# Reciprocal roots by GpSimd's power in a sparse attention, and a later spreading step in feed-forward norms, in a one-core decoder trunk

## Chip, cores and metric

One core of a Trainium2 chip runs the whole program in one launch. The metric is the device time of an execution in microseconds (us), as the median over runs. The engines are TensorE (PE; PEld is its weight load), VectorE (DVE), ScalarE (ACT), GpSimd (POOL) and SyncE (SP), which issues the loads.

## What is computed

A trunk of four layers over 256 tokens of 1024 features, in float32. Each layer is

```python
x = x + 0.5 * swiglu(rmsnorm(x, ffn1_norm[i]), ffn1_w_gu[i], ffn1_w_down[i])
h = rmsnorm(x, mix_norm[i])
x = x + mixer(h)        # 0 gated delta rule, 1 stick-breaking, 2 sparse attention, 0 again
x = x + 0.5 * swiglu(rmsnorm(x, ffn2_norm[i]), ffn2_w_gu[i], ffn2_w_down[i])
# rmsnorm(x, g) = x * rsqrt(mean(x*x) + 1e-6) * g
```

The sparse attention projects `h` to a query latent (384), a key latent (256), a rotary key (32) and an index key (64), and takes an rmsnorm of the query latent, the key latent and the index key. Index scores choose 64 keys of 256 for each query, and a softmax over those keys attends.

## The kernel before, in words

Everything lies transposed, features on the partitions and 256 tokens along the free axis. A float32 product is made of three passes on two-part operands (high part by a copy on ACT, `piece` L172, remainder by a subtraction on DVE, L173), so each 128x128 weight tile costs three matmuls of 256 columns. These are the "products" below. Weights come in chunks of 1 MB, each good for 48 products.

A norm's factor is not needed by the products: they run on `x` times the gain, and the factor of each token is multiplied in afterwards. `rstd` (L241) makes it in three steps: squares on ACT and three and a half additions on GpSimd; two small matmuls with a matrix of ones (the "sum", on PE) with the mean taken by DVE into `ms` (L256), and the reciprocal root `rsqrt` (L205) on DVE, one bit trick and three rounds of Newton's iteration, 10 instructions; then two transposes on PE that spread the two columns of the result over all partitions (`spread`, L234, recorded at `tr`, L56), and a copy of that by ACT to `rb` (L261). `rms_factor` (L749) and `rowbc` (L758) do the same for the three latents of the sparse attention, where one more copy on DVE (L756) puts the result into `fac`.

What is issued when is set by a planner written by hand. A side task (`rstd`, `factor`, `index_scores`, `attend` and so on) is a generator; what it yields is the time until its next step is due, in the planner's own count, which each matmul advances by its columns over 2400 (0.1067 for a product of 256 columns, L47). `pump` (L132) is called after each 6 products of a wide tile (0.64 in the count) and runs the steps that are due; `wait` (L147) runs steps, due or not, until a condition holds. So a yield of 4.6 puts 48 products between the sum and the spreading. Within that order a list scheduler still moves instructions that are not ready by its own estimate.

In a feed-forward stage (`ffn`, L313) 192 products of gate and up come before the first rows of the down projection. The task `rstd` is added at the start, so the sum stands after product 60; the factor is waited for after product 144 (L339). In the first feed-forward stage of all the task is added only after product 48.

In the sparse attention (`dsa`, L762) the norm's factor is waited for after 96 products (L972). Then come three factors: `fk` (index key; its spread row is needed by `index_keys`, L835, whose PE work is at L842), `fq` (query latent; not spread, it scales the index weights at L808) and `fkv` (key latent; its spread row is needed before the keys `K` of L1001). DVE then finds the 64 best keys (`select`, L886: eight rounds of a maximum search) and writes the mask `neg` (L903), for which `attend` (L921) waits.

Of the kernel before, what the change touches and what calls it, by code (L numbers as in the profile page):

```python
# [11 lines left out]
F32 = mybir.dt.float32  # L12
# [5 lines left out]
ALU = mybir.AluOpType  # L18
AX = mybir.AxisListType

P = 128
T = 256
# [13 lines left out]
class Bank:  # L36


    def __init__(self, k, t):
        self.k, self.nc, self.t, self.fresh = k, k.nc, t, True  # L40
# [25 lines left out]
class Trunk:  # L66

    def __init__(self, tc, ctx, a):
        self.tc, self.nc, self.a = tc, tc.nc, a
        nc = self.nc  # L70
        pool = lambda **k: ctx.enter_context(tc.tile_pool(**k))
        self.const = pool(name="const", bufs=1)
        self.raw = pool(name="raw", bufs=3)
        self.hip = pool(name="hi", bufs=10)
        self.lop = pool(name="lo", bufs=10)
        self.wk = pool(name="wk", bufs=2)

        pool(name="gap", bufs=1).tile([P, 8], F32, name="gap")
        self.big = pool(name="big", bufs=8)
        self.ps = pool(name="ps", bufs=4, space=bass.MemoryType.PSUM)  # L80
        self.side, self.now = [], 0.0
        self.act_set("silu_and_others")
        c = self.const
        self.x = c.tile([P, KT, T], F32, name="x")
        self.gains = c.tile([P, 13, KT], F32, name="gains")
        self.ones = c.tile([P, P], F32, name="ones")
        nc.gpsimd.memset(self.ones, 1.0)
        self.ident = c.tile([P, P], F32, name="ident")
        bf = c.tile([P, 2, P], BF16, name="bf")
        self.identb, self.scap = (bf[:, i] for i in range(2))  # L90
        hf = c.tile([P, 3, P], F16, name="hf")
        self.identh, self.identk, self.m1 = (hf[:, i] for i in range(3))
        self.consts = ((self.ident, a["ident"]), (bf, a["bf"]), (hf, a["hf"]))
        self.pad = c.tile([P, T], F32, name="pad")
        nc.gpsimd.memset(self.pad, 0.0)
        self.pcs = [c.tile([P, 2, 3 + T], F32, name="pc%d" % i) for i in range(2)]
        for pc in self.pcs:
            nc.gpsimd.memset(pc[:, :, :3], 0.0)

# [138 lines left out]
            b.tr(b.t[:, i * P:(i + 1) * P], c.to_broadcast([P, P]))  # L238
        return b

    def rstd(self, st):  # L241

        nc = self.nc
        sq = self.b8("sq")
        for j in range(4):
            nc.scalar.activation(sq[:, 2 * j:2 * j + 2], self.x[:, 2 * j:2 * j + 2], AF.Square)  # L246
        nc.gpsimd.tensor_add(sq[:, 0:2], sq[:, 0:2], sq[:, 2:4])  # L247
        nc.gpsimd.tensor_add(sq[:, 0:2], sq[:, 0:2], sq[:, 4:6])
        nc.gpsimd.tensor_add(sq[:, 0:2], sq[:, 0:2], sq[:, 6:8])
        nc.gpsimd.tensor_add(sq[:, 0], sq[:, 0], sq[:, 1])  # L250
        yield self.lat_sum
        b = self.bank()
        for t in range(2):
            b.mm(b.t[:, t * P:(t + 1) * P], sq[:, 0, t * P:(t + 1) * P], self.ones)
        a = self.small("ms", [P, 2])
        nc.vector.tensor_scalar(a, b.v4()[:, :2, 0], 1.0 / D, EPS, op0=ALU.mult, op1=ALU.add)  # L256
        y = self.rsqrt(a, 2)
        yield self.lat_newton
        s = self.spread([y[:, t:t + 1] for t in range(2)])
        rb = self.small("rb", [P, T])  # L260
        nc.scalar.activation(rb, s.t[:, :T], AF.Copy)  # L261
        st["rstd"], st["rb"] = y, rb
# [1 line left out]

    pool_lo = ()
    lag, width, burst = 1.0, 6, 5
    lat_sum, lat_newton = 5.2, 4.6
    dsa_width = 4
    g_key, g_val, g_qry, g_del, g_new, g_inv, g_out, g_mul = 9.0, 6.0, 6.0, 8.0, 2.8, 1.0, 7.5, 1.0
    s_qk, s_sp, s_att = 2.5, 5.5, 1.3  # L270
# [42 lines left out]
    def ffn(self, w, n, first=False, done=None):  # L313
        nc = self.nc
        if first:
            c0, xg = self.first_chunk(w[0, 0], n)
        else:
            c0, xg = None, self.norm_in(n)
        st = {}
        if not first:  # L320
            self.add(self.rstd(st))

        def gu(s):
            for f in range(2):
                order = range(KT) if first and s + f == 0 else None
                c = c0 if c0 and s + f == 0 else self.chunk(w[s, f], parts=4 if first and s == 0 else 1)
                if first and s == 0 and f:
                    for t, src in self.consts:
                        nc.sync.dma_start(t, src)
                e = self.w5("e")  # L330
                for m in range(2):
                    b = self.tile_wide(c, m, order=order)
                    nc.scalar.activation(e[:, m * T:(m + 1) * T], b.t[:, :T], AF.Copy)  # L333
                    nc.vector.tensor_add(e[:, m * T:(m + 1) * T], e[:, m * T:(m + 1) * T], b.t[:, T:])  # L334
                late.append(e)
                if first and s + f == 0:
                    self.add(self.rstd(st))
                if s > 0:
                    self.wait(lambda: "rb" in st)  # L339
                if "rb" in st:  # L340
                    while late:
                        acts.append(act(late.pop(0)))

        def act(e):
            e2 = e.rearrange("p (a b) -> p a b", b=T)
            nc.vector.tensor_mul(e2, e2, st["rb"][:, None, :].to_broadcast([P, 2, T]))  # L346
            nc.scalar.activation(e[:, :T], e[:, :T], AF.Silu)  # L347
            nc.vector.tensor_mul(e[:, T:], e[:, T:], e[:, :T])  # L348
            ah, al = self.w2("ah", F32R), self.w2("al", F32R, "wb")
            self.split(ah, al, e[:, T:])  # L350
            return ah, al

        late, acts = [], []
        self.scale = 0.5
        for s in range(NS):
            gu(s)
            if s == 1:
                acc = [self.bank() for _ in range(4)]
            if s > 0:
                self.rows(acc, self.chunk(w[s - 1, 2]), (acts.pop(0), acts.pop(0)), False)  # L360
        self.rows(acc, self.chunk(w[NS - 1, 2]), acts, True, done)
# [387 lines left out]
    def rms_factor(self, sq, n, ones, out):  # L749

        b = self.bank()
        for t in range(2):
            b.mm(b.t[:, t * P:(t + 1) * P], sq[:, t * P:(t + 1) * P], ones)
        m = self.small("ms", [P, 2])
        self.nc.vector.tensor_scalar(m, b.v4()[:, :2, 0], 1.0 / n, EPS, op0=ALU.mult, op1=ALU.add)
        self.nc.vector.tensor_copy(out, self.rsqrt(m, 2))  # L756

    def rowbc(self, y, r):  # L758
        s = self.spread([y[:, t:t + 1] for t in range(2)])
# [2 lines left out]
    def dsa(self, n):  # L762
        nc, a = self.nc, self.a
# [9 lines left out]
        self.act_set("natural_log_exp_and_others")  # L773
        self.split(wih, wil, wi)
        st, fl = {}, set()
        self.add(self.rstd(st))
        self.width = 12

        lat = self.b8("lat")
# [43 lines left out]
        def factor(name, i, srcs, n, ones, row):  # L823
            if len(srcs) > 1:
                nc.gpsimd.tensor_add(sq[:, srcs[0]], sq[:, srcs[0]], sq[:, srcs[1]])
            if len(srcs) > 2:
                nc.gpsimd.tensor_add(sq[:, srcs[0]], sq[:, srcs[0]], sq[:, srcs[2]])
            yield 1.0 + 0.8 * (len(srcs) - 1)
            self.rms_factor(sq[:, srcs[0]], n, ones, fac[:, i])
            yield self.lat_newton  # L830
            if row is not None:
                self.rowbc(fac[:, i], row)
            fl.add(name)
# [138 lines left out]
        self.wait(lambda: "rb" in st)  # L972
        latents(1, b1)
        self.add(factor("fk", 2, (3,), 64, ones64, fk), 1.5)
        self.add(index_keys())
        latents(0, b0)
        self.add(idx_weights())
        self.pump(1)
        self.add(factor("fq", 0, (0, 1, 2), 384, self.ones, None), 1.5)
        self.add(weights())  # L980
        pieces = self.chunk(a["dsa_qidx"], 1536, 384)
# [6 lines left out]
        self.add(select())  # L988
        latents(2, project(2))
        self.add(factor("fkv", 1, (4, 5), 256, self.ones, fkv), 1.5)  # L990
        project_q(0)
        pieces = self.chunk(a["dsa_uk"], 1536, 384)
# [218 lines left out]
```

## Time and profile before

| what | us |
|---|---|
| median of 3 runs | 2086.51 |
| lowest and highest run | 2069.57, 2087.42 |
| the profiled execution's own time | 2071.74 |
| span of that execution, first to last instruction | 2069.9 |

The profile is of one execution. A row of a timeline gives the start, the duration, engine, line, operation, what is written and read, and in brackets how long the engine had been idle before and what ended that. Equal neighbours are merged, with their count. Ends of matmuls are modelled: neighbouring products overlap in the record, and their spacing is read from their starts.

### The profile page before, as it was taken

To read this page: it belongs to the slowest core of one execution; us is meant where nothing else is said; L and a number is where in the kernel's file an instruction comes from. 1 tells how busy PE (TensorE), PEld (TensorE's weight loads), DVE (VectorE), ACT (ScalarE), POOL (GpSimd) and SP (SyncE) were. 2 spreads that over 40 slices of the span, in tenths; PEclk is the share of its full clock that TensorE was granted. 3 is DMA by queue.
4 is the path that set the end of the run, shared out by engine and by line. 5 is a ranking of instruction groups with operands and counts; after the bars stand their busy time and mean duration, and the time that the engine had idled before them with its cause. 6 is when DMAs were issued, how large, how long until landed. Compare 5 with 4: busy or idle time off the path is not lost.

```text
span 2069.9 us, 43693 instructions
## 1 busy us (share of the span) xinstructions
PE 2006.7 (97%) x17578; PEld 1975.3 (95%) x17578; DVE 1611.2 (78%) x3456; ACT 1306.9 (63%) x2804; POOL 160.6 (8%) x145
## 2 busy tenths in 40 slices
PE   8999899999999999999999998999999998999998
PEld 8999889999999989999999996999999998899998
DVE  7778898866787776877787788877787788988776
ACT  6666776655666666665666664766666667766664
POOL 1001311100000010100010013100010013111000
PEclk9999999999999999999999999999999999999999
DMA  7555223555455554555555542455555542235552
GB/s 260 200 189 182 103 104 127 176 190 185 164 204 197 190 183 146 178 198 196 191 183 201 187 153 79 150 198 201 186 185 202 186 181 105 101 123 181 186 200 86
DMA packets 52619, 353.93 MB, mean 171 GB/s; under 512 B 6976, under 2 KB 7872, under 8 KB 10688
## 3 DMA queue, kind: packets, MB, share of 16 engines
q1 hardware_dynamic: 52128, 350.49, 47.8%
q8 instruction: 137, 2.24, 0.4%
q10 hardware_dynamic: 288, 0.66, 0.1%
q14 instruction: 66, 0.54, 0.1%
HBM read 350.07 MB, written 1.05 MB: 170 GB/s over the span
## 4 chain that ended last, share of the span: by engine, by line
PE 79%; DVE 15%; ACT 4%; issue 2%; POOL 0%; DMA 0%; SPq 0%; ACTq 0%; DVEq 0%; POOLq 0%
PE bankG L43 52%; PE bankA L43 26%; DVE l L173 6%; ACT x L224 1%; PE bankA L56 1%; DVE kT L470 1%; ACT h L172 1%; DVE x L225 1%; DVE rs_t L213 1%; DVE rs_y L214 1%; DVE x L306 1%; DVE rs_t L212 1%; DVE qT L470 0%; DVE e L334 0%; DVE vT L470 0%
## 5 line engine op out<-in xcount | busy, mean ns | idle before, releaser
L43 PE MATMUL bankG<-x,h 128*128 128x256 f32 x7008 | 1256.5, 280 | 10.0 <-ACT x L224 6.8
L173 DVE TENSOR_TENSOR l<-r,h 128x512 fp32r<-128x512 f32 x1328 | 938.2, 713 | 396.7 <-ACT h L172 395.3
L172 ACT ACTIVATE h<-r 128x512 fp32r<-128x512 f32 x1328 | 821.9, 626 | 573.5 <-PE bankG L43 329.6
L43 PEld LDWEIGHTS bankG<-x,h 128*128 128x128 f32 x7008 | 1079.4, 189 | 12.4 <-ACT x L224 7.1
L43 PE MATMUL bankG<-x,l 128*128 128x256 f32 x3504 | 977.5, 279 | 0.0
L43 PEld LDWEIGHTS bankG<-x,l 128*128 128x128 f32 x3504 | 661.9, 189 | 0.2
L43 PE MATMUL bankA<-al,h 128*128 128x256 f32 x1408 | 389.6, 277 | 0.0
L43 PE MATMUL bankA<-ah,h 128*128 128x256 f32 x1408 | 389.6, 277 | 0.0
L43 PE MATMUL bankA<-ah,l 128*128 128x256 f32 x1408 | 389.5, 277 | 0.0
L43 PEld LDWEIGHTS bankA<-al,h 128*128 128x128 f32 x1408 | 265.1, 188 | 0.1
L43 PEld LDWEIGHTS bankA<-ah,h 128*128 128x128 f32 x1408 | 264.3, 188 | 0.1
L43 PEld LDWEIGHTS bankA<-ah,l 128*128 128x128 f32 x1408 | 264.3, 188 | 0.0
L334 DVE TENSOR_TENSOR e<-e,bankG 128x256 f32<-128x256 f32 x352 | 145.3, 413 | 1.8 <-ACT e L333 1.8
L333 ACT ACTIVATE e<-bankG 128x256 f32<-128x256 f32 x352 | 133.7, 380 | 9.1 <-PE bankG L43 8.5
L247 POOL TENSOR_TENSOR sq<-sq 128x512 f32<-128x512 f32 x12 | 15.7, 1304 | 1454.7 <-ACT sq L246 1454.7
L346 DVE TENSOR_TENSOR e<-e,rb 128x512 f32<-128x512 f32 x176 | 119.6, 684 | 0.0
L201 ACT ACTIVATE ah<-e 128x256 fp32r<-128x256 f32 x176 | 72.8, 418 | 23.0 <-DVE e L348 22.7
L347 ACT ACTIVATE e<-e 128x256 f32<-128x256 f32 x176 | 71.2, 405 | 5.8 <-DVE e L346 5.8
L43 PE MATMUL bankG<-oh,h 128*128 128x256 f32 x256 | 73.4, 287 | 0.1
L348 DVE TENSOR_TENSOR e<-e 128x256 f32<-128x256 f32 x176 | 72.8, 418 | 0.5 <-ACT e L347 0.5
L202 DVE TENSOR_TENSOR al<-e,ah 128x256 fp32r<-128x256 f32 x176 | 72.7, 417 | 0.5 <-ACT ah L201 0.5
L43 PE MATMUL bankG<-oh,l 128*128 128x256 f32 x256 | 71.2, 279 | 0.0
(290 smaller groups left out, 1683.7 us busy)
## 6 DMA issues: line engine op xcount, KB each, us to landing
r<-in_ffn SPq DMA_DIRECT2D x262, 1024.0 KB, 4.8
r<-in_gdn_in SPq DMA_DIRECT2D x32, 1024.0 KB, 4.8
r<-in_gdn_out SPq DMA_DIRECT2D x8, 1024.0 KB, 4.7
r<-in_sb_qk SPq DMA_DIRECT2D x8, 1024.0 KB, 4.9
r<-in_sb_v SPq DMA_DIRECT2D x4, 1024.0 KB, 4.8
r<-in_sb_out SPq DMA_DIRECT2D x4, 1024.0 KB, 4.8
r<-in_dsa_out SPq DMA_DIRECT2D x4, 1024.0 KB, 4.8
r<-in_dsa_in SPq DMA_DIRECT2D x3, 1024.0 KB, 4.8
```

The lines of the kernel that those rows point to most:

```text
L43: self.nc.tensor.matmul(out, lhsT, rhs, start=self.fresh, stop=stop, skip_group_check=True)
L56: self.nc.tensor.transpose(out, x, self.k.ident)
L172: self.nc.scalar.activation(h[:, :pw], src, AF.Copy)
L173: (self.nc.gpsimd if pool else self.nc.vector).tensor_sub(l[:, :pw], src, h[:, :pw].bitcast(F32))
L201: self.nc.scalar.activation(dh, src, AF.Copy)
L202: self.nc.vector.tensor_sub(dl, src, dh.bitcast(F32))
L212: nc.vector.tensor_mul(t, y, y)
L333: nc.scalar.activation(e[:, m * T:(m + 1) * T], b.t[:, :T], AF.Copy)
L334: nc.vector.tensor_add(e[:, m * T:(m + 1) * T], e[:, m * T:(m + 1) * T], b.t[:, T:])
L346: nc.vector.tensor_mul(e2, e2, st["rb"][:, None, :].to_broadcast([P, 2, T]))
L347: nc.scalar.activation(e[:, :T], e[:, :T], AF.Silu)
L348: nc.vector.tensor_mul(e[:, T:], e[:, T:], e[:, :T])
```

## The change

`rstd` gets two arguments, the planner's delay between sum and spreading, and whether the root is taken by one GpSimd instruction: `ms` to the power of -0.5, the exponent from two columns of a constant tile. The sparse attention's norm and its three factors use the power, with 2.4 as the delay. All other norms keep Newton's iteration; in the feed-forward stages the delay becomes 6.6 in place of 4.6, elsewhere it stays 4.6. The constant lies behind the data of one of the two convolution tiles, each of which grows by two columns.

```diff
-        self.pcs = [c.tile([P, 2, 3 + T], F32, name="pc%d" % i) for i in range(2)]
+        pcs = [c.tile([P, 2 * (4 + T)], F32, name="pc%d" % i) for i in range(2)]
+        self.pcs = [t[:, :2 * (3 + T)].rearrange("p (m t) -> p m t", m=2) for t in pcs]
+        self.half = pcs[1][:, 2 * (3 + T):]
+        nc.gpsimd.memset(self.half, -0.5)
...
-    def rstd(self, st):
+    def rstd(self, st, lat=4.6, power=False):
...
-        y = self.rsqrt(a, 2)
-        yield self.lat_newton
+        if power:
+            y = self.small("rs_y2", [P, 2])
+            nc.gpsimd.tensor_tensor(y, a, self.half, op=ALU.pow)
+        else:
+            y = self.rsqrt(a, 2)
+        yield lat
...
-    lat_sum, lat_newton = 5.2, 4.6
+    lat_sum, lat_power = 5.2, 2.4
...
-            self.add(self.rstd(st))                  # ffn, twice (L321, L337)
+            self.add(self.rstd(st, 6.6))
...
-        self.nc.vector.tensor_copy(out, self.rsqrt(m, 2))          # rms_factor
+        self.nc.gpsimd.tensor_tensor(out, m, self.half, op=ALU.pow)
...
-        self.add(self.rstd(st))                      # dsa
+        self.add(self.rstd(st, 2.4, True))
...
-            yield self.lat_newton                    # factor
+            yield self.lat_power
```

## Rows read from the trace of the kernel before

**Rows 1.** The page: the busy time of each engine with its share of the span and its instructions; then the busy time of each engine between 400 and 560 us, inside one feed-forward stage (engine, busy us, count; then TensorE's granted clock, the DMA share and GB/s).

```profile
PE 2006.7 (97%) x17578; PEld 1975.3 (95%) x17578; DVE 1611.2 (78%) x3456; ACT 1306.9 (63%) x2804; POOL 160.6 (8%) x145
...
400.00:560.00 160.00, 160.00 (x1360) 160.00 (x1360) 110.95 (x209) 93.78 (x189) 0.00 (x0) 1.00 0.53 186
```

**Rows 2.** The timeline of PE in feed-forward stages: in the second stage the sum, the last product ahead of the spreading and the spreading; then the spreading of the other six.

```profile
383.43 0.60 PE L43 MATMUL bankA<-ones,sq 128*128 128x128 f32 x4
...
389.21 0.28 PE L43 MATMUL bankG<-x,h 128*128 128x256 f32 x1
390.29 0.40 PE L56 MATMUL bankA<-ident,rs_y 128*128 128x128 f32 x2 [0.80 <-DVE rs_y L214]
...
578.53 0.43 PE L56 MATMUL bankA<-ident,rs_y 128*128 128x128 f32 x2 [0.72 <-DVE rs_y L214]
...
867.85 0.40 PE L56 MATMUL bankA<-ident,rs_y 128*128 128x128 f32 x2 [0.79 <-DVE rs_y L214]
...
1049.62 0.43 PE L56 MATMUL bankA<-ident,rs_y 128*128 128x128 f32 x2 [0.71 <-DVE rs_y L214]
...
1343.64 0.40 PE L56 MATMUL bankA<-ident,rs_y 128*128 128x128 f32 x2 [0.46 <-DVE rs_y L214]
...
1525.40 0.43 PE L56 MATMUL bankA<-ident,rs_y 128*128 128x128 f32 x2 [0.72 <-DVE rs_y L214]
...
1891.09 0.40 PE L56 MATMUL bankA<-ident,rs_y 128*128 128x128 f32 x2 [0.80 <-DVE rs_y L214]
```

**Rows 3.** The timeline of DVE in the second feed-forward stage: the mean, and the last of Newton's ten instructions.

```profile
386.88 0.15 DVE L256 TENSOR_SCALAR ms<-bankA 128x2 f32<-128x2 f32 x1
...
389.98 0.16 DVE L214 SCALAR_TENSOR_TENSOR rs_y<-rs_t,rs_y 128x2 f32<-128x2 f32 x1
```

**Rows 4.** What PE waited for in the sparse attention, 1228 to 1300 us, the seven longest: us in total, times, longest.

```profile
PE bankA L56 <- DVE fac L756: 3.3, 1, 3.3
PE bankA L43 <- DVE lat L839: 1.9, 1, 1.9
PE bankG L43 <- DVE l L173: 1.7, 1, 1.7
PE bankA L56 <- DVE p L940: 1.4, 3, 0.7
PE bankA L43 <- DVE qtmp L914: 0.9, 1, 0.9
PE bankG L43 <- DVE K L1001: 0.8, 1, 0.8
PE bankA L56 <- DVE rs_y L214: 0.6, 1, 0.6
```

**Rows 5.** The timeline of PE in the sparse attention: the norm's sum and spreading, `fk`'s sum, the first matmuls of `index_keys`, the sum and the spreading of `fkv`.

```profile
1225.16 0.71 PE L43 MATMUL bankA<-ones,sq 128*128 128x128 f32 x4 [0.22 <-POOL sq L250]
...
1230.71 0.43 PE L56 MATMUL bankA<-ident,rs_y 128*128 128x128 f32 x2 [0.60 <-DVE rs_y L214]
...
1233.73 0.60 PE L43 MATMUL bankA<-tab,sq 128*128 128x128 f32 x4
...
1247.49 1.52 PE L43 MATMUL bankA<-lat,tab 128*128 128x256 f32 x4 [1.86 <-DVE lat L839]
...
1259.34 0.60 PE L43 MATMUL bankA<-ones,sq 128*128 128x128 f32 x4
...
1269.99 0.40 PE L56 MATMUL bankA<-ident,fac 128*128 128x128 f32 x2 [3.27 <-DVE fac L756]
```

**Rows 6.** Three us behind the wait of 1.86 us, by the view of stretches (columns as in rows 1).

```profile
1248.00:1251.00 3.00, 3.00 (x14) 2.81 (x13) 1.71 (x5) 0.00 (x0) 2.34 (x3) 0.51 0.50 156
```

**Rows 7.** The three lines of Newton's iteration proper on DVE between 1227 and 1271 us, grouped by line: count, busy us, mean ns, idle before.

```profile
L213 DVE SCALAR_TENSOR_TENSOR rs_t<-rs_t,ms 128x2 f32<-128x2 f32 x12 | 4.0, 331 | 0.2
L214 DVE SCALAR_TENSOR_TENSOR rs_y<-rs_t,rs_y 128x2 f32<-128x2 f32 x12 | 3.5, 288 | 0.2
...
L212 DVE TENSOR_TENSOR rs_t<-rs_y 128x2 f32<-128x2 f32 x12 | 2.4, 202 | 0.3
```

**Rows 8.** The timeline of DVE in the sparse attention: the means of the norm, of `fk` and of `fkv`, one instruction of `fkv`'s Newton iteration, the start of `select` and its mask.

```profile
1227.59 0.15 DVE L256 TENSOR_SCALAR ms<-bankA 128x2 f32<-128x2 f32 x1
...
1234.37 0.16 DVE L755 TENSOR_SCALAR ms<-bankA 128x2 f32<-128x2 f32 x1
...
1261.17 0.15 DVE L755 TENSOR_SCALAR ms<-bankA 128x2 f32<-128x2 f32 x1
...
1264.31 1.24 DVE L213 SCALAR_TENSOR_TENSOR rs_t<-rs_t,ms 128x2 f32<-128x2 f32 x1
...
1269.76 0.48 DVE L891 TENSOR_TENSOR m<-m,tab 128x128 f32<-128x128 f32 x2
...
1286.59 0.48 DVE L903 SCALAR_TENSOR_TENSOR neg<-m,tab 128x128 bf16<-128x128 f32 x2
```

**Rows 9.** The timeline of POOL around `fkv`: the rotary parts of the queries.

```profile
1260.95 1.43 POOL L915 TENSOR_TENSOR Q<-Q,tab 32x512 f32<-32x512 f32 x1 [6.03 <-PE bankA L43]
1263.74 1.79 POOL L916 TENSOR_TENSOR Q<-Q,qtmp 32x512 f32<-32x512 f32 x1 [1.36 <-DVE qtmp L914]
```

**Rows 10.** POOL's instructions grouped by line: an addition of 256 columns, and the shortest instruction over 128 partitions in several columns.

```profile
L825 POOL TENSOR_TENSOR sq<-sq 128x256 f32<-128x256 f32 x2 | 1.5, 736 | 12.7 <-ACT sq L816 12.7
...
L98 POOL MEMSET pc<- 128x6 f32 x2 | 0.1, 105 | 0.0
```

More of the change, by code (lines that the diff above doesn't have):

```diff
@@ L336, in gu @@
                 if first and s + f == 0:
-                    self.add(self.rstd(st))
+                    self.add(self.rstd(st, 6.6))
                 if s > 0:
@@ L775, in dsa @@
         st, fl = {}, set()
-        self.add(self.rstd(st))
+        self.add(self.rstd(st, 2.4, True))
         self.width = 12
```

## The prediction

> **What bounds the kernel now.** I read the shares of the page first, then a stretch of a feed-forward stage, then what PE waited for, then timelines at each norm. PE is busy 97% of the span, and between 400 and 560 us it is busy for all 160.00 us at full granted clock, with DVE at 110.95 and ACT at 93.78 [rows 1]. So PE sets the pace there, and whatever keeps it idle for a moment is paid in full, unless a later wait is shortened by it. In seven feed-forward stages the one such moment is the norm's spreading: PE stands 0.80, 0.72, 0.79, 0.71, 0.46, 0.72 and 0.80 us for Newton's last instruction [rows 2]. That is 5.00 us. In the sparse attention PE is not fully busy. There a chain goes back and forth between PE, DVE and POOL, and the waits are larger: 3.3 us for `fkv`'s factor, 1.9 for the index key, 1.7 for a weight remainder, 1.4 for the softmax, 0.9 for a query's rotation, 0.8 for a key eviction, 0.6 for the norm [rows 4].
>
> **Feed-forward stages: the later spreading.** In the second stage the sum ends at 383.43 + 0.60 = 384.03, and the 48 products behind it end at 389.21 + 0.28 = 389.49, so one product takes 5.46 / 48 = 0.114 us [rows 2]. Newton's result is there at 389.98 + 0.16 = 390.14, or 6.11 us after the sum; 2.85 of them pass before DVE gets to the mean at 386.88 [rows 3], and the rest is its ten small instructions with the stream's own between them. With 66 products in front, the transposes come 66 x 0.114 = 7.52 us after the sum: 1.4 us later than the result, and the wait is gone. In the planner's count 6.6 / 0.64 gives 11 pumps, which is 66 products, where 4.6 / 0.64 gave 8. The sum stands after product 60, so the spreading comes after product 126, still ahead of the point at 144 where the factor is asked for; 18 products or 2.05 us remain for two transposes, 0.40 us in rows 2, and the copy to `rb`. The gate and up values are multiplied by `rb` only after 144, before and after. So nothing is late next. Nothing new is queued: the same transposes move past 18 products that don't need them, and no load moves.
>
> In the first stage of all, the sum comes after product 108 (48, one pump, then 5.2 / 0.64 or 9 pumps) and the wait at 144 forces the spreading before either delay has run out. I count no change there. Gain of this part: 5.0 us, bounded by 0 (if the scheduler put the transposes where they were) and 5.0.
>
> **The sparse attention: one instruction for eleven.** Removed are ten DVE instructions four times and three copies; the three lines of the iteration proper alone cost DVE 4.0 + 3.5 + 2.4 = 9.9 us [rows 7]. Added are four POOL instructions of two columns and one filling of two columns at the start, 0.105 us for six [rows 10] on an engine that is busy 8% of the span [rows 1]; two longer constant tiles cost nothing. The power itself is nowhere in this trace. From below, POOL's shortest instruction takes 0.105 us [rows 10]; from above, a two-input one of 512 columns took 1.79 [rows 9]; an ordinary one of 256 columns takes 0.74 [rows 10]. I take 0.4, nearer the small end, since there are two columns, and above it, since a power is more than an addition. Below nothing it can't be.
>
> Norm: the sum ends at 1225.87 [rows 5]; DVE, busy with remainders, gives the mean at 1227.74 [rows 8]; 2.4 / 0.64 gives 4 pumps, 24 products, so the transposes come 2.74 us after the sum, at 1228.6. The power has 0.86 us and nothing in front of it on POOL. The wait of 0.60 [rows 5] goes.
>
> `fk`: the sum ends at 1234.33 [rows 5], the mean is there at 1234.53 [rows 8], so 2.5 us are left for the power and the wait for it is nil. The spread key comes some 20 products earlier in the planner's order, and DVE, free of `fq`'s Newton, makes the index key at once. So PE's 1.86 us [rows 5] go. What followed that wait goes too: the granted clock was 0.51 from 1248 to 1251, the 1.2 GHz level, after PE had idled until 1247.49 [rows 5, 6]. 14 products started in those 3 us [rows 6], where 3 / 0.114 = 26 do at full clock: (26 - 14) x 0.114 = 1.4 us lost. Behind the waiting power on POOL stand `fq`'s two additions, some 0.5 us later; `fq`'s sum is not asked for until some 20 products on.
>
> `fkv`: the sum ends at 1259.94 [rows 5], the mean at 1261.32 [rows 8]. POOL is in L915 until 1262.38 [rows 9], so the power ends at 1262.8, against transposes at 1259.94 + 2.74 = 1262.68: the wait of 3.27 us [rows 5] nearly vanishes. But POOL works in order. If the power is placed behind L916, which itself waits for DVE and ends at 1265.53 [rows 9], PE waits about 3.2 us again. No row shows which, so I take 2.0 us of the 3.27. Whatever stands behind the power on POOL (the queries' rotations) waits for the mean as well; `attend` needs them, 20 us later.
>
> Will the end of the stage follow? `neg` is written at 1286.59 + 0.48, at the end of a DVE chain that starts at 1269.76 [rows 8], 17 us of almost gapless DVE work. It starts earlier by what DVE saves in front of it and by the earlier index key, about the same 6 us as PE. So I move the rest along: neither the 1.7 nor the 1.4 of rows 4 goes or grows.
>
> Sum: 0.60 + 1.86 + 1.4 + 2.0 = 5.9 in the sparse attention and 5.0 in the feed-forward stages, 10.9 us. Against the profiled execution's own 2071.74 (1.84 outside its span of 2069.9) that is 2060.8. The median of the runs shown is 2086.51, 14.8 above that execution and 17 above the lowest run. I carry the saving over: 2086.5 - 10.9 = **2075.6 us**.
>
> *A rule against it.* DVE's instruction at 1264.31 took 1.24 us where its like takes 0.16 [rows 3], and it ended with POOL's L916, at 1265.5 [rows 8, 9]. The Trainium skill, "SBUF — State Buffer", section "Who interferes with whom", says that a DVE instruction with two SBUF inputs and a GpSimd instruction that reads SBUF exclude each other, the later one waiting in full. The trace agrees in this row. By the rule each power can be held up by DVE, and hold DVE up in turn; with the 1.08 us of this row at `fkv`, the one place without room, the sum would be 9.8 in place of 10.9.
>
> **Rivals.**
>
> *DVE takes it back.* The mask's 17 us chain [rows 8] does not start earlier, since it needs the scores, whose multiplications share DVE with the weights' remainders; PE then arrives earlier and waits longer for keys, remainders and softmax. For it: three of the seven waits in rows 4 are of that kind already, 3.9 us. Against: Newton stands between the last scores. Only the 5.0 remain: 2081.5.
>
> *All of it falls.* The index key comes so early that scores and selection run beside the projections, and all seven waits of rows 4, 10.6 us, go with the 1.4 of the clock: 17.0 with the 5.0, 2069.5. Against it: the softmax waits have nothing to do with the factors.
>
> *The planner's delay does nothing in the feed-forward stages*, because the scheduler places the transposes as before. Against: 48 products stood there as planned [rows 2]. 2086.5 - 5.9 = 2080.6.
>
> *Slower: a dear power.* The price sits at three spreadings, with room of 0.86, 2.5 and 1.36 us between mean and transposes. At p us each PE waits 3p - 4.7. Against it stand 5.0 and the waits removed, 0.60 + 1.86 + 1.4 + 3.27, 12.1 in all: slower from p = 5.6, three times the longest row of rows 9. At p = 8 it is 7 us slower, 2093.7.
>
> **How the numbers follow.** Forecast 0.53, DVE takes it back 0.21, all falls 0.15, nothing in feed-forward 0.07, dear power 0.04. About 1% is what a measurement of this kernel can tell from no change, and none of the first four saves as much as that (20.9 us). But the runs shown lie 17.85 us apart, and two of the four times shown lie near 2070: if the changed kernel's median fell there, the forecast would read 2060.8, 1.2% below. I give that 0.3 of the first three cases. So faster 0.28, same 0.68, slower 0.04. The range goes from 2055, the full gain seen from the low end, to 2088, no gain at the upper.
>
> **What would show it.** Feed-forward: no wait before the spreading, 66 products between it and the sum in seven stages, and Newton's ten unchanged. Sparse attention: four powers on POOL of about 0.4 us each; no wait of 1.9 us at L842's matmuls and no 1.2 GHz after it; `fkv`'s transposes within 1 us of the last product; `neg` some 6 us earlier within the stage. Wrong, if powers take over 1 us, if waits at `L1001`, `L173` and `p` grow by what the others lose, or if the feed-forward stages still show waits.

## The result, and the profile after

The changed kernel takes 2067.78 us (median of 20 runs, 2059.05 to 2077.25), the kernel before in the same comparison 2086.49 (20 runs, 2069.57 to 2101.84). The ratio is 0.9929, with a 95% interval of 0.9911 to 0.9947: 14.8 us less (11 to 18.6). The forecast was 10.9 us less, 2075.6 us, in a range of 2055 to 2088. In a second comparison the same kernel (after_again below) had 0.9905 (0.9874 to 0.9936).

The page after: span, and busy time, share and instructions of each engine.

```profile
span 2064.6 us, 43653 instructions
...
PE 2009.8 (97%) x17578; PEld 1978.6 (96%) x17578; DVE 1603.2 (78%) x3413; ACT 1305.8 (63%) x2804; POOL 163.8 (8%) x150
```

DVE has 43 instructions fewer and POOL five more, as the diff says. The profiled execution is only 5.3 us shorter than that of before. Why it is not 11 shorter is read further down, from the spacing of its products.

The second feed-forward stage after, on PE: the sum, the last product ahead of the spreading, and the spreading; it answers to the first three rows of [rows 2].

```profile
381.39 0.60 PE L43 MATMUL bankA<-ones,sq 128*128 128x128 f32 x4
...
389.21 0.28 PE L43 MATMUL bankG<-x,h 128*128 128x256 f32 x1
389.32 0.38 PE L56 MATMUL bankA<-ident,rs_y 128*128 128x128 f32 x2
```

There is no idle time in brackets: 7.3 us pass from the end of the sum to the transposes, and on DVE Newton's last instruction ended before them:

```profile
387.94 0.16 DVE L217 SCALAR_TENSOR_TENSOR rs_y<-rs_t,rs_y 128x2 f32<-128x2 f32 x1
```

The same holds in the other six stages. The sparse attention after, on PE, answers to [rows 5]: the norm's sum and spreading, `fk`'s sum and spreading, the first matmuls of `index_keys`, its last ones, and `fkv`'s sum and spreading.

```profile
1221.26 0.71 PE L43 MATMUL bankA<-ones,sq 128*128 128x128 f32 x4 [0.37 <-POOL sq L253]
...
1225.05 0.43 PE L56 MATMUL bankA<-ident,rs_y 128*128 128x128 f32 x2 [0.34 <-POOL rs_y L262]
...
1233.77 0.61 PE L43 MATMUL bankA<-tab,sq 128*128 128x128 f32 x4
...
1236.80 0.38 PE L56 MATMUL bankA<-ident,fac 128*128 128x128 f32 x2
...
1240.20 1.10 PE L43 MATMUL bankA<-lat,tab 128*128 128x256 f32 x4 [1.18 <-DVE lat L846]
...
1244.41 0.67 PE L43 MATMUL bankA<-m,tab 128*128 128x256 f32 x2 [0.55 <-DVE m L856]
...
1255.47 0.61 PE L43 MATMUL bankA<-ones,sq 128*128 128x128 f32 x4
...
1259.35 0.43 PE L56 MATMUL bankA<-ident,fac 128*128 128x128 f32 x2 [1.35 <-POOL fac L763]
```

The norm's wait fell from 0.60 to 0.34 us, `fkv`'s from 3.27 to 1.35, the index key's only from 1.86 to 1.18, with a new 0.55 behind it. The powers on POOL, grouped by line (count, busy us, mean ns, idle before):

```profile
L763 POOL TENSOR_TENSOR fac<-ms,pc 128x2 f32<-128x2 f32 x3 | 2.1, 700 | 13.0 <-DVE ms L762 13.0
L262 POOL TENSOR_TENSOR rs_y<-ms,pc 128x2 f32<-128x2 f32 x1 | 1.1, 1079 | 2.7 <-DVE ms L259 2.7
```

A power takes 0.70 us, not the 0.4 of the estimate; the norm's took 1.08.

Whole stages are read from the first product of each. First the kernel before (the sparse attention, the next stage, and the one after that), then the kernel after (the same three):

```profile
1220.32 0.50 PE L43 MATMUL bankG<-x,h 128*128 128x256 f32 x2 [0.37 <-DVE x L225]
...
1332.45 0.50 PE L43 MATMUL bankG<-x,h 128*128 128x256 f32 x2 [0.28 <-DVE x L225]
...
1514.31 0.50 PE L43 MATMUL bankG<-x,h 128*128 128x256 f32 x2 [0.37 <-DVE x L225]
```

```profile
1216.42 0.50 PE L43 MATMUL bankG<-x,h 128*128 128x256 f32 x2 [0.37 <-DVE x L228]
...
1323.27 0.50 PE L43 MATMUL bankG<-x,h 128*128 128x256 f32 x2 [0.44 <-DVE x L228]
...
1504.14 0.50 PE L43 MATMUL bankG<-x,h 128*128 128x256 f32 x2 [0.37 <-DVE x L228]
```

The feed-forward stage went from 181.86 to 180.87 us, and the sparse attention from 112.1 to 106.85.

### The profile page after: what moved, and what is told of

It reads as the page before. It is cut to its first block, busy times and chain, and to the rows that moved or that the text cites. A ratio compares the mean times of both kernels' runs of the same rounds, so it can differ in the third digit from the quotient of the medians.

```text
span 2064.6 us, 43653 instructions
## 1 busy us (share of the span) xinstructions
PE 2009.8 (97%) x17578; PEld 1978.6 (96%) x17578; DVE 1603.2 (78%) x3413; ACT 1305.8 (63%) x2804; POOL 163.8 (8%) x150
## 4 chain that ended last, share of the span: by engine, by line
PE 83%; DVE 11%; ACT 3%; issue 2%; POOL 1%; DMA 0%; SPq 0%; ACTq 0%; DVEq 0%; POOLq 0%
PE bankG L43 56%; PE bankA L43 26%; DVE l L176 4%; ACT x L227 1%; DVE kT L477 1%; PE bankA L56 1%; ACT h L175 1%; DVE x L228 1%; DVE qT L477 0%; DVE x L313 0%; DVE rs_y L217 0%; DVE vT L477 0%; DVE pc L466 0%; DVE rs_t L215 0%; ACT sq L249 0%
## 5 line engine op out<-in xcount | busy, mean ns | idle before, releaser
L176 DVE TENSOR_TENSOR l<-r,h 128x512 fp32r<-128x512 f32 x1328 | 936.2, 713 | 398.9 <-ACT h L175 396.8
```

Of the source, the lines that this page charges most:

```text
L176: (self.nc.gpsimd if pool else self.nc.vector).tensor_sub(l[:, :pw], src, h[:, :pw].bitcast(F32))
```

## The spacing of products, which moves a run by several times these terms

The reader can count PE's matmuls in equal stretches inside feed-forward stages (columns as in [rows 1]). First the kernel before, in its second such stage and in the one that runs at 880 us, then the kernel after in the same two.

```profile
400.00:550.00 150.00, 150.00 (x1275) 150.00 (x1275) 103.42 (x194) 87.16 (x176) 0.00 (x0) 1.00 0.54 189
880.00:1030.00 150.00, 150.00 (x1326) 150.00 (x1325) 107.53 (x203) 91.24 (x185) 0.00 (x0) 1.00 0.55 194
```

```profile
400.00:550.00 150.00, 150.00 (x1326) 150.00 (x1325) 108.28 (x204) 91.31 (x185) 0.00 (x0) 1.00 0.56 197
880.00:1030.00 150.00, 150.00 (x1276) 150.00 (x1276) 105.46 (x200) 88.16 (x179) 0.00 (x0) 1.00 0.53 190
```

PE has no idle time and its full granted clock in all four. Yet 150 us hold 1275 or 1276 matmuls in the one stage and 1326 in the other, 117.6 against 113.1 ns, and the two kernels have it the other way round. A feed-forward stage has about 1580 products. In the seven later ones the spacing changes only where PE has stood idle, at the stage's first products and, in kernels with the wait, at the spreading; from there it stays to the end, and at the wider one the stage is 6.6 to 6.9 us longer. [Rows 1] shows such a stretch too, 1360 in 160 us, and I read it as PE's pace without asking whether it was the only one.

The profile before had one of eight feed-forward stages at the wider spacing, the profile after two. Taken off at 6.6 and 6.9 us, the spans are 2063.3 and 2050.8: 12.5 us apart. A second profile of the changed kernel (after_again) comes to 2054.3, so this measure is good to some 3.5 us. This is how the kernels are compared below, beside their ratios:

| kernel | ratio to before (95%) | span | stages at 118 ns | span without them | sparse attention |
|---|---|---|---|---|---|
| before | | 2069.9 | 1 | 2063.3 | 112.1 |
| after | 0.9929 (0.9911 to 0.9947) | 2064.6 | 2 | 2050.8 | 106.8 |
| after_again | 0.9905 (0.9874 to 0.9936) | 2074.9 | 3 | 2054.3 | 107.5 |
| ffn_only | 0.9958 (0.9932 to 0.9985) | 2081.6 | 4 | 2054.2 | 110.6 |
| dsa_only | 1.0006 (0.9977 to 1.0034) | 2083.6 | 4 | 2056.9 | 106.8 |
| dsa_newton_early | 0.9970 (0.9944 to 0.9996) | 2067.7 | 1 | 2061.1 | 110.0 |
| dsa_power_late | 1.0001 (0.9975 to 1.0027) | 2079.4 | 3 | 2059.5 | 108.9 |

Stages and spacings are worked out from the starts of the matmuls in each trace. Each comparison has its own runs of the kernel before, whose median went from 2079.1 to 2090.0 us between comparisons, so only ratios are compared across them. The lowest times point the same way: 2065.28 us for the kernel before in all comparisons, 2054.13 for the kernel after, 11.2 us less.

## The experiments

**ffn_only**: the feed-forward delay alone.

```diff
-            self.add(self.rstd(st))
+            self.add(self.rstd(st, 6.6))     # both places in ffn; Newton everywhere
```

> The kernel before, with only the delay of the feed-forward norms' spreading changed (66 products in front, Newton kept everywhere). Theory A (the two parts add, each by the waits it removes): no wait of PE at the spreading in the seven later feed-forward stages, 5.0 us less, ratio 0.9976, and the sparse attention unchanged at 112 us from its first product to that of the next stage. Theory B (the spreading's wait also decides in which of two spacings, 113 or 118 ns, a feed-forward stage runs its products afterwards; one stage of eight was at 118 in the profile before, two in the one after): fewer stages at 118 ns than in the kernel before, each worth 6.8 us, so a gain well over 5, some 9 us or more, ratio 0.9957 or lower.

Measured: 2067.83 us against 2079.94, 0.9958 (0.9932 to 0.9985). In its second stage PE's only wait is the first product's:

```profile
PE bankG L43 <- DVE x L225: 0.4, 1, 0.4
```

Stages at 113 ns take 180.8 to 180.95 us where the kernel before has 181.7 to 181.9. So theory A's waits are gone, and each is worth 0.9 us rather than the 0.72 of its idle time: 6.5 for seven. The gain of 8.7 us (3 to 14) is above A and at B's edge, but the profile shows four stages at 118 ns and not fewer. In the feed-forward stages what shows is A, with a larger term.

Two other stages changed, which A did not expect. The stick-breaking attention, which nothing was done to, took 108.8 us, and 109.0 in the kernel after, where the kernel before takes 107.2. Its own norm makes PE wait for Newton, 2.16 us in each. First the kernel before, the wait and three us behind it, then the kernel after:

```profile
760.85 0.43 PE L56 MATMUL bankA<-ident,rs_y 128*128 128x128 f32 x2 [2.16 <-DVE rs_y L214]
...
761.00:764.00 3.00, 3.00 (x15) 2.49 (x15) 1.20 (x3) 2.52 (x5) 0.00 (x0) 1.00 0.59 246
```

```profile
750.38 0.43 PE L56 MATMUL bankA<-ident,rs_y 128*128 128x128 f32 x2 [2.16 <-DVE rs_y L217]
...
751.00:754.00 3.00, 3.00 (x9) 2.35 (x8) 0.69 (x1) 1.41 (x4) 0.00 (x0) 0.50 0.41 172
```

After the same wait the granted clock stays at 1.00 in the one and is 0.50, the 1.2 GHz level, for 3.4 us in the other. The four profiles with the waits of 48 products and Newton in this norm have no such stretch here, and all seven profiles with 54 products or more and Newton in this norm have it. So the later spreading gives 6.5 us in seven stages and loses 1.6 to 1.8 in this one. Why the clock falls only there, after an equal wait, no run shows.

And the sparse attention took 110.6 us and not 112.1, with its three longest waits as before. There it is the other way round, with the clock at 1.00 behind the wait for the index key:

```profile
1249.82 1.10 PE L43 MATMUL bankA<-lat,tab 128*128 128x256 f32 x4 [1.87 <-DVE lat L839]
...
1250.00:1253.00 3.00, 3.00 (x24) 2.90 (x23) 1.71 (x4) 0.65 (x2) 2.70 (x4) 1.00 0.42 98
```

The kernel before had 0.51 and 14 matmuls in such a stretch [rows 6]. So that wait does not always bring the lower clock.

**dsa_only**: the powers with the delay of 2.4, and the feed-forward spreading back at 48 products.

```diff
-            self.add(self.rstd(st, 6.6))
+            self.add(self.rstd(st, 4.6))     # both places in ffn
```

> The kernel after, with the feed-forward norms' spreading back at 48 products; the sparse attention has its four powers and the delay of 2.4. Theory A: the seven waits of 0.46 to 0.80 us are there again, the sparse attention takes 107 us in place of 112; 5.3 us less than before, ratio 0.9975. Theory B (spacing): the same waits, and as many stages at 118 ns as before, so the whole of the gain beyond 5.3 us is missing; the two alike here, B alone would need ffn_only to be far above 5.

Measured: 1.0006 (0.9977 to 1.0034), so the 5.3 us did not show in the time, a miss by the ratio. In the profile they are there: the sparse attention takes 106.8 us, and the spreading's waits are back (the second and third feed-forward stages):

```profile
PE bankA L56 <- DVE rs_y L217: 1.5, 2, 0.8
```

Four stages of eight ran at 118 ns, which is 26.7 us. In three of the four, the spacing was 113 ns up to the spreading and 118 from there on.

**dsa_newton_early**: the order without the power.

```diff
-        self.add(self.rstd(st))              # dsa
+        self.add(self.rstd(st, 2.4))
...
-            yield self.lat_newton            # factor
+            yield 2.4
```

> The kernel before, with the sparse attention's norm and factors still by Newton's iteration, but with their delay at 2.4 in place of 4.6. It tells the order apart from the power. If the earlier place of the spreading is what gains (the index key's turn in the order), the sparse attention falls by 3 us or more from 112. If it is DVE's relief (11.9 us of Newton's instructions), PE waits longer at the norm's spreading (1.5 us or more in place of 0.60) and at fkv's, and the stage takes 112 us or more.

Measured: 0.9970 (0.9944 to 0.9996), and a sparse attention of 110.0 us. What PE waited for in it, longest first:

```profile
PE bankA L56 <- DVE fac L756: 4.6, 2, 2.8
PE bankA L56 <- DVE p L940: 1.7, 3, 1.0
PE bankA L56 <- DVE rs_y L214: 1.5, 1, 1.5
```

The norm's wait is 1.5 as expected, the factors' have grown to 4.6, and the index key's is gone. The stage is 2.1 us shorter than in the kernel before, but only 0.6 shorter than in ffn_only, which like this one has no stretch at 1.2 GHz there: what the order gains it pays at the spreadings for Newton.

**dsa_power_late**: the power without the order.

```diff
-    lat_sum, lat_power = 5.2, 2.4
+    lat_sum, lat_power = 5.2, 4.6
...
-        self.add(self.rstd(st, 2.4, True))
+        self.add(self.rstd(st, 4.6, True))   # and ffn back at 4.6
```

> The kernel after, with the feed-forward spreading at 48 products and the sparse attention's powers kept, but their delay at 4.6 as before. If DVE's relief is what gains, the stage takes about 107 us, as with 2.4. If the earlier place in the order is needed, the index key's matmuls come as late as before, the wait of 1.9 us stays in part, and the stage takes 109 to 111 us.

Measured: 1.0001 (0.9975 to 1.0027), and a sparse attention of 108.9 us, just under the 109 to 111 that the second reading expects. Its largest waits:

```profile
PE bankG L43 <- DVE K L1008: 4.5, 1, 4.5
PE bankA L43 <- DVE neg L910: 1.5, 1, 1.5
PE bankA L43 <- DVE lat L846: 1.0, 1, 1.0
```

With the power in time but its spreading late, PE waits 4.5 us for the keys, which need `fkv`'s row. Behind that wait the clock falls again:

```profile
1271.00:1274.00 3.00, 3.00 (x16) 3.00 (x16) 3.00 (x14) 0.63 (x1) 0.00 (x0) 0.54 0.00 0
```

By the starts of its products that costs some 1.5 us. At equal clock, against the 110.6 of ffn_only, the power alone then gives some 3 us, the order alone 0.6 and both together 3.8. So nearly all of it is the power; the second reading's number came in part from the clock. These are single profiles, and the same program's stage took 106.8 and 107.5 in two of them.

**after_again**: the kernel after, once more.

> The kernel after, once more. From the profiles so far, a feed-forward stage at 113 ns takes 181.8 us with the wait and 180.9 without, and the sparse attention 110.6 to 112.1 in kernels with Newton and 106.8 with the power: 10 to 12 us less than before when as many stages run at 118 ns, ratio 0.9945. If the spacing theory held (fewer stages at 118 ns without the wait), 0.992 or lower. In the profile, no stage changes its spacing at the spreading, since there is no wait.

Measured: 2066.75 us against 2086.88, ratio 0.9905 (0.9874 to 0.9936). That is below the 0.9945 that the terms give, and under the 0.992 that the spacing theory asked for. But its profile has three stages at 118 ns, not fewer, so it doesn't show that theory right. None of the seven later stages changes its spacing at the spreading.

**fq_pool**: whether `fq`'s power holds the index key up.

```diff
-            nc.vector.tensor_mul(w2, w2, fac[:, 0, :, None].to_broadcast([P, 2, 8]))
-            nc.vector.tensor_scalar(scl, fac[:, 0], P ** -0.5, None, op0=ALU.mult)
+            nc.gpsimd.tensor_mul(w2, w2, fac[:, 0, :, None].to_broadcast([P, 2, 8]))
+            nc.gpsimd.tensor_scalar(scl, fac[:, 0], P ** -0.5, None, op0=ALU.mult)
```

The reason is seen in the kernel after: on POOL the two rotations of `qi` and then `fq`'s power, on DVE the wait for that power, and the index key behind it.

```profile
1235.32 0.73 POOL L871 TENSOR_TENSOR qi<-qi,tab 96x256 f32<-96x256 f32 x1
1236.13 0.73 POOL L872 TENSOR_TENSOR qi<-qi,rtmp 96x256 f32<-96x256 f32 x1
1236.82 0.70 POOL L763 TENSOR_TENSOR fac<-ms,pc 128x2 f32<-128x2 f32 x1
...
1237.55 0.70 DVE L815 TENSOR_TENSOR wx<-wx,fac 128x16 f32<-128x16 f32 x1 [1.80 <-POOL fac L763]
...
1239.04 1.01 DVE L846 SCALAR_TENSOR_TENSOR lat<-lat,dg,fs 128x256 f32<-128x256 f32 x1
```

> The kernel after, with the two small instructions that use fq's power (L815, L816) moved from DVE to GpSimd; DVE's order is otherwise the same. Theory: in the kernel after, fq's power stands behind two rotations on GpSimd, DVE stands 1.80 us at L815 for it, and the index key (L846), queued behind L815, makes PE wait 1.18 us. Then here DVE's wait is gone and PE's wait at the index key falls to 0.4 us or less. Rival: the index key waits for its own spread row and for ports held by GpSimd; then PE's wait stays at 1 us or more.

Measured: one time of 2071.58 us, and 109.2 us for the sparse attention (107.5 in after_again, the kernel that it edits). The wait at the index key is gone, as the theory says, but another has grown, PE's longest in the stage:

```profile
PE bankA L43 <- DVE m L856: 2.1, 1, 2.1
```

That is the last link of the same chain. On POOL, its two rotations (L854, L855) stand behind everything else:

```profile
1238.93 0.70 POOL L763 TENSOR_TENSOR fac<-ms,pc 128x2 f32<-128x2 f32 x1
1239.71 0.43 POOL L815 TENSOR_TENSOR wx<-wx,fac 128x16 f32<-128x16 f32 x1
...
1243.63 0.74 POOL L854 TENSOR_TENSOR lat<-lat,tab 64x256 f32<-64x256 f32 x1
1244.44 0.72 POOL L855 TENSOR_TENSOR lat<-lat,tab 32x256 f32<-32x256 f32 x1
```

So DVE's wait was one link and POOL's queue, without a gap of 0.1 us from 1236.8 to 1246, is the bound: the expected gain turned into a wait one step further on. The two waits of this chain grew only from 1.7 to 2.1 us. Most of the rest is the clock, which falls behind the new wait and does not in the kernel after:

```profile
1248.00:1251.00 3.00, 3.00 (x16) 3.00 (x16) 1.05 (x3) 0.68 (x2) 0.00 (x0) 0.50 0.50 153
```

**power_twice**: the price of a power.

```diff
             nc.gpsimd.tensor_tensor(y, a, self.half, op=ALU.pow)
+            nc.gpsimd.tensor_tensor(y, a, self.half, op=ALU.pow)     # and so in rms_factor
```

> The kernel after, with each of the four powers issued twice, so that a power costs 1.4 us or so in place of 0.70. It tells how much room there is behind each. If the room worked out before holds (0.86 us at the norm, 2.5 at fk, 1.36 at fkv), PE's wait at the norm's spreading grows from 0.34 by 0.7 to 1.0, at fkv's from 1.35 by 0.7 to 2.1, and the stage from 106.8 by about 1.5 to 2 us. If the power is free beside other work, nothing grows.

Measured: one time of 2071.51 us. PE's waits at the norm, the index key and `fkv`:

```profile
1227.61 0.43 PE L56 MATMUL bankA<-ident,rs_y 128*128 128x128 f32 x2 [1.02 <-POOL rs_y L263]
...
1244.24 2.04 PE L43 MATMUL bankA<-lat,tab 128*128 128x256 f32 x4 [2.69 <-DVE lat L848]
...
1264.92 0.43 PE L56 MATMUL bankA<-ident,fac 128*128 128x128 f32 x2 [2.11 <-POOL fac L765]
```

They grew by 0.68, 1.51 and 0.76, and the stage from 106.8 to 110.2. The second power took 0.70 each time, so norm and `fkv` pay it in full, as expected. At the index key the growth is that of two powers (`fk`'s and `fq`'s), where the prediction had seen 2.5 us of room. Behind the wait of 2.69 us the clock was at 0.52 from 1244 to 1247 us, so the stage's 3.4 us are not waits alone.

**norms_power**: the power in all norms, the feed-forward spreading back at 48 products.

```diff
-            self.add(self.rstd(st, 6.6))
+            self.add(self.rstd(st, 4.6, True))   # ffn twice; gdn and sb likewise
...
-            r = self.rsqrt(a, 2)                 # final
+            r = self.small("rs_y2", [P, 2])
+            nc.gpsimd.tensor_tensor(r, a, self.half, op=ALU.pow)
```

> The kernel after, with the power also in the norms of the feed-forward stages (delay back at 4.6, 48 products), of the delta rule, of the stick-breaking attention and of the output. If the power shortens what the spreading waits for (the mean 2.85 us after the sum, 0.7 to 1.1 for the power, against 5.5 us of products), no wait at the feed-forward spreadings although 48 products are back; the waits of 0.6 to 0.9 at the delta rule's norm go, those of 2.2 at the stick-breaking attention's and the output's fall to about 1. Some 4 us less than the kernel after at equal spacing. Rival: the power's wait behind other GpSimd work takes it back; then the waits stay at 0.5 us or more.

Measured: 1.0204 (1.0158 to 1.0250), 42 us slower than before, against all expectation. The feed-forward waits are gone, as expected; but every stage ran wide:

```profile
400.00:550.00 150.00, 150.00 (x1266) 150.00 (x1266) 105.21 (x199) 88.02 (x180) 0.00 (x0) 1.00 0.53 188
```

That is 118.5 ns, and all feed-forward stages took 189 to 193 us. With the last use of `rs_t2` gone, its two tiles were not allocated any more, and every tile behind them lay 64 bytes lower.

**norms_power_layout**: the same, with that tile back.

```diff
             y = self.small("rs_y2", [P, 2])
+            self.small("rs_t2", [P, 2])          # not used
```

> norms_power with one unused tile (rs_t2, two columns, twice) allocated again, so that every tile behind it lies where it lies in the kernel after; norms_power had them 64 bytes lower and ran all its products 118.7 ns apart on the mean. Theory (the place of the tiles set that spacing, the power did not): products at 113.4 ns again in most feed-forward stages, the waits as in norms_power (none at the feed-forward spreadings, 1.7 at the stick-breaking attention's, 1.0 at the output's), some 2 us less than the kernel after at equal spacing, ratio to before 0.993 or so. Rival (GpSimd's power or its 43 fewer DVE instructions change the stream): all stages at 189 us as in norms_power, ratio 1.02.

Measured: 2057.46 us against 2079.12, 0.9931 (0.9897 to 0.9965). All eight stages of its profile are at 113 ns:

```profile
400.00:550.00 150.00, 150.00 (x1326) 150.00 (x1326) 108.19 (x205) 91.50 (x187) 0.00 (x0) 1.00 0.55 193
```

The place of the tiles had cost 69 us of span (2125.0 against 2055.6). The power at 48 products also removes the feed-forward waits. But the two delta-rule stages took 186.7 and 186.4 us, where the kernel after took 183.5 and 183.7 and the other kernels with Newton there 182.5 to 185.9. Their spreading now waits 1.5 us and not 0.6 to 0.9:

```profile
203.72 0.43 PE L56 MATMUL bankA<-ident,rs_y 128*128 128x128 f32 x2 [1.52 <-POOL rs_y L263]
```

**ffn_54** and **ffn_84**: other delays in the feed-forward norms.

```diff
-            self.add(self.rstd(st, 6.6))
+            self.add(self.rstd(st, 5.2))         # ffn_54; 8.4 in ffn_84
```

> The kernel after, with a delay of 5.2 in the feed-forward norms: 54 products between sum and spreading. Newton's result was there 6.11 us after the sum; 54 products take 54 x 0.1134 = 6.12. Expected: no wait, or one under 0.2 us, at the seven spreadings; stages at 113 ns take 180.9 to 181.0 us. If the wait is longer than 0.2, the result comes later than worked out.

> The kernel after, with a delay of 8.4: 84 products between sum and spreading, which then stands just where the factor is asked for (product 144). Expected if the factor's own readiness is all that counts: no wait, stages at 180.9 us as with 66. If the multiplications by rb are late next (they are issued from product 144 on and the first rows need them at 192): a wait of up to 1 us at the first rows, stages at 181 to 182 us.

Measured: one time each, 2074.46 and 2061.24 us. With 54 products the waits are 0.1 us, and stages at 113 ns take 181.1 to 181.2; with 84 there is no wait, and they take 180.8 to 180.95, as with 66. Any place from 54 or so up to 84 would do, and what comes behind `rb` is not late even there. The stick-breaking stage takes 108.9 and 109.0 us, with the clock's fall, in both.

**sb_out_power**: the kernel after, with the power where norms_power_layout gained.

```diff
-        self.add(self.rstd(st))                  # sb
+        self.add(self.rstd(st, 4.6, True))
...
-            r = self.rsqrt(a, 2)                 # final
+            r = self.small("rs_y2", [P, 2])
+            nc.gpsimd.tensor_tensor(r, a, self.half, op=ALU.pow)
```

> The kernel after, with the power also in the norm of the stick-breaking attention (delay 4.6) and in the output's, and nowhere else; all tiles lie as in the kernel after. From the stages of norms_power_layout: the stick-breaking stage 107.1 us in place of 109.0, the last stage 184.1 in place of 185.3 at 113 ns; 3.1 us less than the kernel after at equal spacing, some 15 less than the kernel before, ratio 0.9925, with the delta-rule stages at 183 to 184 as in the kernel after and not 186.4. If the power's gain there is taken back later in the stage, the two stages take what they took.

Measured: 2064.59 us against 2090.04, 0.9891 (0.9838 to 0.9944). The stick-breaking stage takes 107.2 us and the last one 184.1, as expected; one stage of eight was at 118 ns. Of the 1.8 us in the stick-breaking stage some 1.5 are the clock, which stays at 1.00 there, and the wait is 0.3 shorter: the stage is only back where it was in the kernel before, with Newton. It is faster than the kernel before. That it beats the kernel after shows in the two stages only; the ratios' intervals overlap.

## Why the prediction was right, and which of its terms were off

*Feed-forward stages: right in the mechanism, and right in the sum by luck.* 66 products, no wait, nothing late in these stages. The term was 5.0 and measures 6.5: the idle time in brackets is not all that a wait costs, since a stage lost 0.9 us where PE stood 0.71 on average. But "nothing is late next" looked only at the stage itself. In the stick-breaking attention behind, the granted clock fell to 0.50 after a wait that had been harmless, and 1.8 us went (shown under ffn_only). The net is 4.7, near the 5.0 by two misses.

*Sparse attention: right in its sum, 5.9 against 5.3, by terms that erred both ways.* `fkv`'s 2.0 measured 1.9. The norm gave 0.26 and not 0.60, the power being dearer than 0.4. The clock's 1.4 us came: no stretch at 1.2 GHz is left in this stage. But that it came from the index key's wait, as the prediction has it, is not shown: in ffn_only that wait stands and the clock stayed at 1.00. With `fk` below, these terms make 3.7. The rest came from rows that the prediction left alone: the wait for a weight remainder fell from 1.7 to 0.5 us and the key eviction's 0.8 went, while the queries' rotation grew from 0.9 to 1.6. Without the clock, against the 110.6 of ffn_only, the stage gains 3.8.

*The mis-sized step is `fk`.* It was to give 1.86 us and gave 0.13 (1.18 and 0.55 are left). The step said that DVE, free of `fq`'s Newton, makes the index key at once. But `fq`'s power has a place in POOL's order, behind two rotations, and DVE, in order too, stood 1.80 us at the instruction that uses it, ahead of the index key. In fq_pool that wait went and the chain's next link waited 2.1 us for POOL; in power_twice the index key's wait grew by two powers.

*A term put at nothing without a row: "two longer constant tiles cost nothing".* The prediction gives no reason, and norms_power shows that the place of tiles alone can cost 69 us. Here it probably did hold: two unused tiles of 8 bytes made 64 bytes there, so room seems to be taken in steps of 32 bytes, and by this estimate the old 2072 and the new 2080 bytes of a convolution tile take the same place. No trace shows the addresses; the traces show both spacings in the kernel after as in ffn_only, whose tiles are those of before.

*The rule on shared ports.* The norm's power took 1.08 us, and 1.08 again in the repeats, where the others took 0.70. Remainders on DVE (L176, two inputs) were under way, the first with 0.52 us left when the power began at 1223.91:

```profile
1223.76 1.28 DVE L176 TENSOR_TENSOR l<-r,h 128x512 fp32r<-128x512 f32 x2
```

The power was longer by 0.38 of these 0.52 us. In norms_power_layout eleven of the twelve powers that began in that position took 1.08 or 1.09 us and one 1.68; the four that met no such remainder under way took 0.70. This agrees, to 0.14 us, with the Trainium skill, "SBUF — State Buffer", section "Who interferes with whom", under which the later of the two waits in full. What does not show is the other direction: the second remainder of the row, begun while the power ran, took its usual 0.68. In power_twice the second of the norm's powers, behind the first, took 0.69.

*The rivals.* "DVE takes it back" fell: `neg` is written 12 us earlier within the stage, by the traces' starts (1270.6 against a stage start of 1216.4, before 1286.6 [rows 8] against 1220.3), twice what I allowed. The stage is only 5.3 shorter all the same: PE is busy for 98 of its 106.85 us, the wait for the rotation grew and the softmax's 1.4 stayed. "A dear power" holds in its mechanism, with no room at all, but 0.70 is far below the 5.6 that decides.

*What stays open.* By stages the traces account for 6.5 + 5.3 - 1.8 = 10 us, and by the spans without wide stages for 12.5 and 9.0 in two profiles. The ratios say 14.8 (11 to 18.6) and 19.8 (13 to 26), the second above all of these. Nor do the two parts alone add up to it: ffn_only gave 8.7 us and dsa_only nothing. The difference may lie in how many stages of a run have the wide spacing: medians above the spans without it would leave some three for the kernel before and two for the kernel after. In the profiles the share is the same: of the seven later stages, 8 of 28 end wide in four profiles with the wait, 11 of 42 in six with 66 products. What is shown, for these seven stages, is that in kernels with the wait a stage can change its spacing at the spreading, either way, while without it none did. In the first stage of all it changed behind the spreading after a wait of under 0.1 us, in ffn_only and power_twice. That the change makes wide stages rarer is not shown.

## What to carry to other kernels

When the wait is for a small result and the waiting engine has other work in its order, move the consumer by as many instructions as the result takes, and read the room from the trace; here any place from 54 to 84 products was about as good. Handing a chain of small instructions to an idle engine moves it into that engine's queue: look for who stands in front of it there, and for who, in order, stands behind the one that waits for it. And before comparing two profiles, compare the spacing of equal instructions and the granted clock of every stage, untouched ones too, since both may differ by more than the change.

## What was not expected of the hardware

At full granted clock and without idle time, a matmul of 256 columns follows the last after 113 or after 118 ns, for a whole stage of 180 us and differently from one execution to the next; after and after_again are the same program, and not the same stages of theirs are wide. With the tiles behind `rs_t2` 64 bytes lower it was 118.5 ns in every stage, 69 us of the span. Which of the operands' places matters, and what chooses the spacing at the start of a stage, was not tried.

A wait of 2.16 us on TensorE was followed by 3.4 us at the 1.2 GHz level in seven profiles and by none in four, by whether small waits in the stages before it had been removed. What links them is not known.
